# Activation-stationary up projections, two-pass down projections and seven block products for eight in a two-layer fp32 trunk

## The chip, the cores and the metric

The kernel runs on one core of a Trainium2 chip. The metric is the device time of one execution in microseconds (us), as the median of several runs. In the profile PE is TensorE (PEld its weight loads), DVE is VectorE, ACT is ScalarE, POOL is GpSimd and SP is the engine that issues the DMAs. L113 is line 113 of the kernel shown.

## The reference, cut to what matters

Two post-norm layers over 256 positions of 2048 features, all in float32. Layer 0 mixes tokens with a spatial gate (gMLP), layer 1 with latent attention. Each is followed by a gated MLP with a width-3 causal convolution over positions.

```python
def layer_norm(x, g, b):          # over features, in float32
def gmlp_mixer(x, w_in, ln_g, ln_b, w_s, b_s, w_out):
    z = jax.nn.gelu(x @ w_in)                    # 2048 -> 2 * 6144
    u, v = jnp.split(z, 2, axis=-1)
    v = layer_norm(v, ln_g, ln_b)
    ...                                          # s: 128-position windows of v, mixed by masked w_s, plus b_s
    return (u * s.reshape(B, S, GM_HALF)) @ w_out
def conv_ffn(x, w_up, conv_w, conv_b, w_down):
    h = x @ w_up                                 # 2048 -> 2 * 5504
    h = lax.conv_general_dilated(h, ...) + conv_b  # each feature: 3 taps over positions, causal
    a, g = jnp.split(h, 2, axis=-1)
    return (jax.nn.silu(g) * a) @ w_down         # 5504 -> 2048
for i in range(DEPTH):
    m = gmlp_mixer(x, ...) if i % 2 == 0 else mla_mixer(x, ...)
    x = layer_norm(ALPHA * x + m, ...)
    x = layer_norm(ALPHA * x + conv_ffn(x, ...), ...)
```

## The kernel before, in words

Every large product runs as three float32r matmuls. A float32 operand t is split into hi = t rounded to float32r and lo = t - hi; the kernel sums hi·hi, hi·lo and lo·hi. Activations x are split once per layer into four tiles `xhl` ([128 features, 4 blocks, 256 hi + 256 lo positions]). Weights stream from DRAM: class `Feed` holds the list of all weight chunks in their order of use (1 MB each, 128 x 2048). For each, `_load` issues a DMA on SP into a tile `raw`, `_split` makes `wh` with a cast on ScalarE (L75) and `wl` with a subtraction on VectorE (L76), in halves of 1024. `next` is called by the consumer and first brings loads and splits a given number of chunks ahead. All these tiles share one pool `big` of 22 buffers of 8 KB per partition.

The products have two forms. In `prod_b` the activations are the stationary operand and the weights stream, 512 columns at a time; the result is [128 positions, features]. In `prod_a` a 128x128 piece of the weights is stationary and the activations stream: first hi and lo side by side (512 columns) against `wh`, then hi (256 columns) against `wl`; the result is [128 features, positions]. PSUM has eight banks of 128x512, given out in turn.

The stages in order: `v` (six groups of 1024 columns in form b, Gelu, layer norm statistics); `u` (twelve groups of 512 columns in form a, each followed by `gate`, which adds the two halves of a bank, applies Gelu, mixes `v` by a small product `s`, and multiplies); `wo` (`down`: 48 blocks of k, form b, all eight banks as accumulators, both halves of the positions and all 2048 columns); `ffn` of layer 0: `upf` (the first 512 columns, form b, interleaved with the layer norm in `boundary`), then `up` (20 groups of 512 columns in form a, which hold 256 columns of a and the matching 256 of g, and a last half-size group), with `pair` making the convolution, Silu and product for one feature block at a time; `dn` (`down` again, 43 blocks); then the attention; then `ffn` and `dn` of layer 1. The last blocks of k of a `down` are held back (`late`, SKEW) and done bank by bank, so that the layer norm of the first half can run beside them.

Each engine runs its instructions in one written order. A scheduler sets it at build time, engine by engine, from the program and its data dependencies; on the chip it is fixed.

## Time and profile before

| | |
|---|---|
| median of 3 runs | 2559.76 us (2559.61 to 2564.33) |
| the profiled execution | span 2559.8 us |
| PE / DVE / ACT busy | 99% / 61% / 48% |
| granted TensorE clock, mean | 0.998 |
| DMA, mean | 188 GB/s, 52% of the 16 engines' time |
| chain by tile | `up` 36%, `dn` 18%, `u` 10%, `v` 10%, `wo` 10% |

Each row of a group or a timeline names line, engine, operation, output and inputs. The busy time of matmuls is modelled, since they overlap; the distance from one start to the next tells what one costs in a sequence.

### The profile page before, as it was taken

To read this page: it belongs to the slowest core of one execution; us is meant where nothing else is said; L and a number is where in the kernel's file an instruction comes from. 1 tells how busy PE (TensorE), PEld (TensorE's weight loads), DVE (VectorE), ACT (ScalarE), POOL (GpSimd) and SP (SyncE) were. 2 spreads that over 40 slices of the span, in tenths; PEclk is the share of its full clock that TensorE was granted. 3 is DMA by queue.
4 is the path that set the end of the run, shared out by engine and by line. 5 is a ranking of instruction groups with operands and counts; after the bars stand their busy time and mean duration, and the time that the engine had idled before them with its cause. 6 is when DMAs were issued, how large, how long until landed. Compare 5 with 4: busy or idle time off the path is not lost.

```text
span 2559.8 us, 32217 instructions
## 1 busy us (share of the span) xinstructions
PE 2544.2 (99%) x13041; PEld 2152.4 (84%) x13041; DVE 1573.6 (61%) x2284; ACT 1226.4 (48%) x1795; POOL 2.4 (0%) x15
## 2 busy tenths in 40 slices
PE   9999999999999999999999999999999999999998
PEld 7888888888888888888888888877888888888886
DVE  6444675575546766665675547845676576667554
ACT  5434444455443555544554433544365455446441
POOL 0000000000000000000000000000000000000000
PEclk9999999999999999999999999999999999999999
DMA  8545454556563545544565554424555454446552
GB/s 323 194 165 197 165 181 165 181 211 230 200 231 148 214 173 188 182 171 175 198 222 205 205 203 159 165 99 154 191 198 181 163 199 174 184 169 242 206 205 87
DMA packets 68838, 480.18 MB, mean 188 GB/s; under 512 B 7633, under 2 KB 8273, under 8 KB 11729
## 3 DMA queue, kind: packets, MB, share of 16 engines
q1 hardware_dynamic: 68688, 478.13, 52.0%
q8 instruction: 102, 1.67, 0.3%
q14 instruction: 48, 0.39, 0.0%
HBM read 476.00 MB, written 2.10 MB: 187 GB/s over the span
## 4 chain that ended last, share of the span: by engine, by line
PE 99%; DVE 1%; DMA 0%; ACT 0%; issue 0%; SPq 0%; DVEq 0%; ACTq 0%
PE up L113 36%; PE dn L113 18%; PE u L113 10%; PE v L113 10%; PE wo L113 10%; PE mo L113 4%; PE upf L113 2%; PE sc L113 1%; PE mkv L113 1%; PE qn L113 1%; PE kn L113 1%; PE vv L113 1%; PE mq L113 1%; PE s L113 1%; PE qr L113 0%; PE lnt L366 0%
## 5 line engine op out<-in xcount | busy, mean ns | idle before, releaser
L76 DVE TENSOR_TENSOR wl<-raw,wh 128x1024 fp32r<-128x1024 f32 (+2 forms) x886 | 1050.6, 1214 | 473.3 <-ACT wh L75 294.1
L75 ACT CAST wh<-raw 128x1024 fp32r<-128x1024 f32 (+2 forms) x886 | 891.0, 1044 | 523.9 <-DVE wl L76 202.8
L113 PE MATMUL up<-xhl,wh 128*128 128x512 f32 x2624 | 927.5, 399 | 0.0
L113 PE MATMUL up<-xhl,wl 128*128 128x256 f32 x2624 | 737.6, 281 | 0.0
L113 PEld LDWEIGHTS up<-xhl,wh 128*128 128x128 f32 x2624 | 493.5, 188 | 122.6
L113 PEld LDWEIGHTS up<-xhl,wl 128*128 128x128 f32 x2624 | 496.5, 189 | 0.1
L113 PE MATMUL u<-xhl,wh 128*128 128x512 f32 x768 | 268.8, 397 | 0.0
L113 PE MATMUL u<-xhl,wl 128*128 128x256 f32 x768 | 212.2, 279 | 0.0
L113 PE MATMUL v<-wh,xhl 128*128 128x512 f32 x768 | 208.2, 392 | 1.8 <-ACT wh L75 1.8
L113 PE MATMUL wo<-wh,woa 128*128 128x512 f32 x768 | 194.5, 390 | 0.0
L113 PE MATMUL dn<-wh,dn1a 128*128 128x512 f32 x688 | 174.2, 389 | 0.0
L113 PE MATMUL dn<-wh,dn0a 128*128 128x512 f32 x688 | 173.5, 390 | 0.0
L113 PEld LDWEIGHTS v<-wh,xhl 128*128 128x128 f32 x768 | 145.1, 189 | 33.1 <-ACT wh L75 2.3
L113 PEld LDWEIGHTS u<-xhl,wh 128*128 128x128 f32 x768 | 143.5, 188 | 32.8
L113 PEld LDWEIGHTS wo<-wh,woa 128*128 128x128 f32 x768 | 144.1, 188 | 29.8
L113 PEld LDWEIGHTS dn<-wh,dn0a 128*128 128x128 f32 x688 | 129.1, 188 | 26.8
L113 PEld LDWEIGHTS dn<-wh,dn1a 128*128 128x128 f32 x688 | 129.1, 188 | 26.7
L113 PEld LDWEIGHTS u<-xhl,wl 128*128 128x128 f32 x768 | 144.7, 188 | 1.1
L113 PE MATMUL v<-wl,xhl 128*128 128x512 f32 x384 | 119.0, 391 | 0.0
L113 PE MATMUL wo<-wl,woa 128*128 128x512 f32 x384 | 107.0, 390 | 0.0
L113 PE MATMUL dn<-wl,dn1a 128*128 128x512 f32 x344 | 96.0, 389 | 0.0
L113 PE MATMUL dn<-wl,dn0a 128*128 128x512 f32 x344 | 95.2, 390 | 0.0
(204 smaller groups left out, 2113.5 us busy)
## 6 DMA issues: line engine op xcount, KB each, us to landing
raw<-in_ffn_up_dram SPq DMA_DIRECT2D x172, 1024.0 KB, 4.8
raw<-in_gm_in_dram SPq DMA_DIRECT2D x95, 1024.0 KB, 4.7
raw<-in_ffn_dn_dram SPq DMA_DIRECT2D x86, 1024.0 KB, 4.7
raw<-in_gm_wout_dram SPq DMA_DIRECT2D x48, 1024.0 KB, 4.8
raw<-in_ml_out_dram SPq DMA_DIRECT2D x16, 1024.0 KB, 4.8
raw<-in_ml_b_dram SPq DMA_DIRECT2D x14, 1024.0 KB, 4.9
raw<-in_ml_kv_dram SPq DMA_DIRECT2D x5, 864.0 KB, 4.7
lng<-in_ln_rows_dram SPq DMA_DIRECT2D x4, 1024.0 KB, 6.3
```

The lines of the kernel that those rows point to most:

```text
L75: self.nc.scalar.copy(hi[:, c], raw[:, c])
L76: self.nc.vector.tensor_tensor(lo[:, c], raw[:, c], hi[:, c].bitcast(F32), ALU.subtract)
L113: nc.tensor.matmul(o, l, r, start=start, stop=stop, skip_group_check=True)
```

## The change

The weights now come as `Step`s of two blocks of k by 1024 columns, and `square` computes a 1024-column group with activations stationary in four accumulator banks (two halves of the positions by two of the columns). This covers `v`, `u` (six groups instead of twelve) and the 20 groups of `up` (now ten of 1024, hence ten groups per layer numbered 0 to 9). `u` and `up` then have their results in [positions, features], and TensorE transposes them: 16 transposes a group, into banks `uT` or `ht`. The convolution takes two feature blocks of a and two of g at once: 12 scaled copies on ScalarE from PSUM, then two shifted additions of 4 x 255 and 4 x 254 columns on VectorE (`conv3`).

`down` makes two passes over k, one for each half of the columns, the second in reverse order; activations are split again where the second pass needs them. The residual is kept in DRAM meanwhile (`park`, `residual`).

In 115 steps (tables GROUP_V, GROUP_U, GROUP_UP, SEVEN_WO, SEVEN_DN: 15 in `v`, 12 in `u`, 40 in `up`, 16 in `wo`, 32 in both `dn`) the 2x2 by 2x2 block product is done with seven block products by sums of blocks (Winograd's form of Strassen's). Sums of the activations are made once (`sums2`, VectorE, then cast and subtraction); sums of the weights (`wt`) for each step. So such a step has the tiles `wh`, `wl` (1536 columns) and `th`, `tl` (2048). Four more banks `p` gather the products that serve several outputs; `gather` and `out` add them up in a tile `h` or `u`.

```diff
+    def _split(self):
+        ...
+        if s.seven:
+            cols = 1536
+            t = self._tile("wt")
+            last = raw[:, 1536:2048].rearrange("p (n c) -> p n c", n=1).to_broadcast([P, 2, 512])
+            nc.vector.tensor_tensor(t[:, 0:1024]..., raw[:, 512:1536]..., last, ALU.subtract)          # L92
+            t1, b22 = (t[:, 512:1024], raw[:, 512:1024]) if s.by_k else (t[:, 0:512], raw[:, 1024:1536])
+            nc.vector.tensor_tensor(t[:, 1024:1536], b22, t1, ALU.add)                                # L95
+            nc.vector.tensor_tensor(t[:, 1536:2048], raw[:, 0:512], t[:, 1024:1536], ALU.subtract)    # L96
-        step = 512 if i == 0 else 1024 if cols == 2048 else cols // 2
+        step = 512 if self.split == 0 else cols
         for o in range(0, cols, step):
             c = slice(o, o + step)
+            nc.scalar.copy(s.hi[:, c], raw[:, c])                                                     # L100
+            nc.vector.tensor_tensor(s.lo[:, c], raw[:, c], s.hi[:, c].bitcast(F32), ALU.subtract)     # L101
+        if s.seven:
+            s.th, s.tl = self._tile("th", F32R), self._tile("tl", F32R)
+            nc.scalar.copy(s.th, t)                                                                   # L104
+            nc.vector.tensor_tensor(s.tl, t, s.th.bitcast(F32), ALU.subtract)                         # L105
...
+TWO = ((0, False), (1, False), (2, True), (4, False), (3, True), (5, False), (6, False), (7, False))
+THREE = ((0, False), (2, True), (1, False), (3, True), (5, False), (4, True), (6, False), (7, False))
+GROUP_V = [NONE] + [THREE] * 5
+GROUP_U = [TWO] * 6
+GROUP_UP = [TWO] * 10
+SEVEN_WO = tuple(range(8, 40, 4))
+SEVEN_DN = tuple(range(8, 40, 4))
...
+            direct(0, 0, x_parts(xs, k0, 0), w(0, 0))          # Square.step, seven: each line 3 matmuls
+            direct(0, 1, sp(3), w(0, 1))
+            self.mm3(self.p[0], first, x_parts(xs, k1, 0), w(1, 0))
+            self.mm3(self.p[1], first, sp(0), t(o1))
+            self.mm3(self.p[3], first, sp(2), t(o3))
+            self.mm3(self.p[2], first, sp(1), t(1024))
+            direct(1, 0, x_parts(xs, k0, 1), t(1536))
...
+    def conv3(layer, tiles, name):
+        c = [tp.tile([P, 4, S], F32, tag="mid", name=f"c{i}_{name}", bufs=MID) for i in range(3)]
+        for i, (F, src) in enumerate(tiles):
+            nc.scalar.activation(c[0][:, i], src, AF.Identity, bias=..., scale=...)                   # L701
+            nc.scalar.activation(c[1][:, i], src, AF.Copy, scale=...)                                 # L702
+            nc.scalar.activation(c[2][:, i], src, AF.Copy, scale=...)                                 # L703
+        y = c[0][:, 0:n]
+        nc.vector.tensor_tensor(y[:, :, 1:S], y[:, :, 1:S], c[1][:, 0:n, 0 : S - 1], ALU.add)         # L705
+        nc.vector.tensor_tensor(y[:, :, 2:S], y[:, :, 2:S], c[2][:, 0:n, 0 : S - 2], ALU.add)         # L706
...
+        for half in range(2):                                   # down
+            order = back_order(n_k, half)
+            ...
+                feed.room = BIG - 8 - (3 if sevens else 0) - (2 if half else 0) + (i // 4 if half else 0)
```

How the change orders the helpers, at three places. First VectorE around the end of an `up` group in layer 0. Before, the parts for one feature block (`h_`, `c_`, `act`) stand between halves of weight splits (`wl`):

```order
L205 TENSOR_TENSOR h_0a_6850<-up_2_0_6684,lo_0a_6848 128x256
L76 TENSOR_TENSOR wl_7011<-raw_6936,wh_7010 128x1024
L461 SCALAR_TENSOR_TENSOR c_0a_6852<-h_0a_6850,cst,c_0a_6852 128x255
L205 TENSOR_TENSOR h_0g_6858<-up_2_2_6686,lo_0g_6856 128x256
L463 SCALAR_TENSOR_TENSOR c_0a_6852<-h_0a_6850,cst,c_0a_6852 128x254
L76 TENSOR_TENSOR wl_7011<-raw_6936,wh_7010 128x1024
```

After, at the end of group 3 (L405 is the drain of the group's last bank, 14 and 16 are the feature blocks; `wt`, `wl`, `tl` are those of the seven step that comes third in group 4):

```order
L405 TENSOR_TENSOR h_3_7195<-h_3_7195,up_3_1_1_7025 128x512
L705 TENSOR_TENSOR c_0_14_7309<-c_0_14_7309,c_0_14_7310 128x4x255
L706 TENSOR_TENSOR c_0_14_7309<-c_0_14_7309,c_0_14_7311 128x4x254
L718 TENSOR_TENSOR act_1_6681<-s_14_7326,c_0_14_7309 128x512
L705 TENSOR_TENSOR c_0_16_7339<-c_0_16_7339,c_0_16_7340 128x4x255
L706 TENSOR_TENSOR c_0_16_7339<-c_0_16_7339,c_0_16_7341 128x4x254
L718 TENSOR_TENSOR act_2_7356<-s_16_7357,c_0_16_7339 128x512
L92 TENSOR_TENSOR wt_7366<-raw_7237 128x1024
L95 TENSOR_TENSOR wt_7366<-raw_7237,wt_7366 128x512
L101 TENSOR_TENSOR wl_7365<-raw_7237,wh_7364 128x1536
L96 TENSOR_TENSOR wt_7366<-raw_7237,wt_7366 128x512
L105 TENSOR_TENSOR tl_7373<-wt_7366,th_7372 128x2048
```

Both convolutions stand ahead of the weight sums and of the seven step's `wl`. Next ScalarE at the same place. Before, each copy or convolution start alternates with half a weight cast:

```order
L203 COPY lo_0a_6848<-up_2_0_6684 128x256
L75 CAST wh_7010<-raw_6936 128x1024
L460 ACTIVATE c_0a_6852<-h_0a_6850,cst 128x256
L203 COPY lo_0g_6856<-up_2_2_6686 128x256
L75 CAST wh_7010<-raw_6936 128x1024
L460 ACTIVATE c_0g_6860<-h_0g_6858,cst 128x256
```

After, the end of the 24 scaled copies of group 3, then the seven step's casts (`s_16` is the second Silu):

```order
L701 ACTIVATE c_0_16_7339<-ht_3_1_1_7330,cst 128x256
L702 ACTIVATE c_0_16_7340<-ht_3_1_1_7330,cst 128x256
L703 ACTIVATE c_0_16_7341<-ht_3_1_1_7330,cst 128x256
L717 ACTIVATE s_16_7357<-c_0_16_7339 128x512
L100 CAST wh_7364<-raw_7237 128x1536
L104 CAST th_7372<-wt_7366 128x2048
L100 CAST wh_7403<-raw_7268 128x2048
```

The cast `wh_7364` stands behind the second Silu, which needs VectorE's adds. Last, VectorE within `wo`. Before, two weight halves and one activation split (`woa`) for each block of k:

```order
L76 TENSOR_TENSOR wl_5193<-raw_5128,wh_5192 128x1024
L212 TENSOR_TENSOR woa_5154<-pT_2881,woa_5154 128x256
L76 TENSOR_TENSOR wl_5193<-raw_5128,wh_5192 128x1024
L76 TENSOR_TENSOR wl_5228<-raw_5163,wh_5227 128x1024
L212 TENSOR_TENSOR woa_5189<-pT_2881,woa_5189 128x256
```

After, in the second pass, one seven step (five rows of `wt`, `wl`, `tl`) and one plain one, with the split of four blocks of activations:

```order
L92 TENSOR_TENSOR wt_5168<-raw_5057 128x1024
L95 TENSOR_TENSOR wt_5168<-raw_5057,wt_5168 128x512
L101 TENSOR_TENSOR wl_5167<-raw_5057,wh_5166 128x1536
L96 TENSOR_TENSOR wt_5168<-raw_5057,wt_5168 128x512
L105 TENSOR_TENSOR tl_5175<-wt_5168,th_5174 128x2048
L101 TENSOR_TENSOR wl_5179<-raw_5088,wh_5178 128x2048
L92 TENSOR_TENSOR wt_5238<-raw_5139 128x1024
L299 TENSOR_TENSOR woa_5_5233<-v_936,woa_5_5233 128x4x256
```

The `tl` stands directly behind the last row of its `wt`, with ScalarE's cast `th` between them.

## The prediction

> **What bounds the kernel now.** I read the page first, then TensorE's waits, the chain in order of time, the groups by shape, and short stretches of the timelines.

> ```profile
> span 2559.8 us, 32217 instructions
> PE 2544.2 (99%) x13041; PEld 2152.4 (84%) x13041; DVE 1573.6 (61%) x2284; ACT 1226.4 (48%) x1795; POOL 2.4 (0%) x15
> ```

> ```profile
> PE v L113 <- ACT wh L75: 1.8, 1, 1.8
> PE o L113 <- ACT pts L681: 1.5, 1, 1.5
> ```

> TensorE is never late: its longest waits are 1.8 and 1.5 us in the whole span. So time is the sum of its instructions, and VectorE (61%) and ScalarE (48%) only have to be early. The profiled span, 2559.8 us, is within 0.1 us of the median of the runs, 2559.76, so I sum against it.

> The chain gives what each kind of matmul takes when they follow one another (start, length, what):

> ```profile
> 98.70 174.13 PE v L113 x768
> 855.93 457.92 PE up L113 x2592
> 1313.86 231.21 PE dn L113 x1020
> 843.49 0.44 PE lnt L366 x4
> ```

> With activations stationary (`v`, `dn`) one 512-column matmul takes 174.13/768 = 231.21/1020 = 0.2267 us. With weights stationary (`up`) a pair, 512 and 256 columns, takes 457.92/1296 = 0.3533, against 1.5 x 0.2267 = 0.3400 for the same columns in the other form. A 128x128 transpose takes 0.11.

> The helpers' prices are distances from one start to the next, VectorE first, then ScalarE:

> ```profile
> 571.65 0.42 DVE L437 TENSOR_TENSOR pT<-u,sg 128x256 f32<-128x256 f32 x1
> 571.99 1.22 DVE L76 TENSOR_TENSOR wl<-raw,wh 128x1024 fp32r<-128x1024 f32 x1
> 573.12 0.41 DVE L212 TENSOR_TENSOR woa<-pT,woa 128x256 fp32r<-128x256 f32 x1
> ...
> 821.28 0.69 DVE L343 BATCH_NORM_STATS2 lnst<-res 128x6 f32<-128x512 f32 x1
> 821.88 0.73 DVE L355 SCALAR_TENSOR_TENSOR res<-res,lnrs,lnb 128x512 f32<-128x512 f32 x1
> ```

> ```profile
> 855.75 0.56 ACT L460 ACTIVATE c_0a<-uph,cst 128x256 f32<-128x256 f32 x1 [5.28 <-PE uph L490]
> 856.22 0.56 ACT L460 ACTIVATE c_0g<-uph,cst 128x256 f32<-128x256 f32 x1
> ...
> 862.55 0.42 ACT L476 ACTIVATE s<-c_0g 128x256 f32<-128x256 f32 x1
> 862.87 1.99 ACT L75 CAST wh<-raw 128x1024 fp32r<-128x1024 f32 x2
> ...
> 872.14 1.06 ACT L75 CAST wh<-raw 128x1024 fp32r<-128x1024 f32 x1
> 873.09 0.60 ACT L460 ACTIVATE c_0a<-h_0a,cst 128x256 f32<-128x256 f32 x1
> 873.60 0.36 ACT L203 COPY lo_0g<-up 128x256 f32<-128x256 f32 x1
> 873.85 1.06 ACT L75 CAST wh<-raw 128x1024 fp32r<-128x1024 f32 x1
> ```

> VectorE: 0.34 us for 256 columns, 0.60 for 512, 1.13 for 1024, so by the line through them 1.67 for 1536 and 2.2 for 2048. ScalarE: 0.95 for a cast of 1024, so 1.4 and 1.8 for 1536 and 2048; Identity of 256 from PSUM 0.47, a plain copy of 256 0.25, Silu 0.32 (0.54 for 512 by the casts' slope). The new scaled copies of 256 have no row; the plain copy bounds them below, the Identity above. I take 0.33.

> **TensorE's own work.** A seven step takes 7 block products of 3 matmuls where a plain one takes 8: 115 x 3 = 345 fewer, -78.2 us. All of `u` (768 pairs) and 2 x 1280 pairs of `up` change form: 3328 x (0.3533 - 0.3400) = -44.3. Their results are now [positions, features] and have to be turned: 16 transposes in each of 6 `u` and 20 `up` groups, 416 x 0.11 = +45.8. Net -76.7. If nothing waited, 2483.

> **What the helpers must now do.** A plain step (two blocks of k) gives TensorE 24 x 0.2267 = 5.44 us and costs VectorE 2.2. A seven step gives 21 x 0.2267 = 4.76 and costs VectorE, for `wt`, `wl`, `tl`: 1.13 + 0.60 + 0.60 + 1.67 + 2.2 = 6.2, and `tl` must wait until ScalarE has cast the finished `wt` (1.8). On average this fits, but both queues run in their written order, and what counts is who is late at a seven step.

> **Up groups, 10 per layer.** Take the end of group 3 (the order above), t = 0 at its last matmul. VectorE's four drains end at 1.5; the turned banks stand at about 1.7 to 2.3. ScalarE then makes 12 scaled copies for the first two pairs of features (4 x 0.47 + 8 x 0.33 = 4.4): 6.1. VectorE's two shifted adds (1020 columns, 1.13 each): 8.5. Silu, product: 9.8. The last 8 of the next 12 copies had to wait for Silu: 12.2. Adds 14.5, Silu 15.1. Only now comes the cast of the seven step's `wh` (1.4): 16.5, while VectorE ends its product and `wt` at 17.5 and `wl` (1.67) at 19.2. TensorE has done its transposes and the two plain steps, 2.3 + 10.7, at 13.0: it waits about 6 us for `wl`, then about 2 for `th`, the next cast and `tl`. With 0.5 at the drains the group takes 8.6 us more than its work. Groups 5 and 7 stand in the same order; group 1 has a 2.2 us `wl` between its drains too: 10.0. In groups 0 and 2 `wt` comes ahead of the adds and `wl` between the two pairs: 2.3 at the drains and 1.4 at the seven step, 3.7 each. In 4 and 6 `wl` stands ahead of all adds: 1.0 each; group 8: 2.0. The first group waits 2.5 for the same chain on the held-back tiles. After the last, the tail product covers until 13.5, but the down pass's first activations are cast behind that chain, both tail copies and two weight casts, at 21.5: 8.9 with its drains. Sum per layer 35.8 + 7.4 + 2.0 + 2.0 + 2.5 + 8.9 = 58.6; both 117. With the copies at 0.25 and every second-order wait left out it is 76, with 0.47 and one late load per group 135.

> **Down projections.** Six half passes, each with eight seven steps alternating with plain ones: TensorE 10.2 us a pair; VectorE 6.2 + 2.2 + 1.13 (a split of activations each pair) + 1.3 (sums every second) = 10.9, and 1.8 idle for `th` unless other work stands there. The order shows such fillers in about half of the places: 12 a pair. Seven pairs behind the first owe 7 x 1.8 = 13, of which about 8 lie after the last `wl`: 5 a half, 30 together. With every place filled it is 7 x 0.7 less the lead, some 1.5 a half or 9; with none and no overlap of two seven steps 13 or 80. I stay near the low end, since half of the places are seen to be filled.

> **`v`, `u`, start.** `v` needs 37 us of VectorE for 41.5 of TensorE; its room shrinks by a buffer each group and only the last (the seven step's split stands behind the drain) waits, about 4, the rest 1, the start 2: +7 (2 to 15). `u` groups cover their seven steps (TensorE has 5.3 us of transposes and `s` products ahead of two plain steps): 0.5 each. But the first stands behind

> ```profile
> L411 DVE TENSOR_SCALAR v<-v,vmv,vrs 128x1024 f32<-128x1024 f32 x12 | 8.8, 804 | 0.0
> ```

> 12 x 0.73: `wl` at 17.9 where TensorE is ready at 10.9: 7. Together +10 (5 to 15). The boundaries gain a head start by the first pass and lose nothing I can see: 0. Parking the residual in DRAM moves 2 MB a time beside a DMA load of half the span: 0 (to +5).

> **The clock.** TensorE's waits may cost beyond themselves. The stretches (length, busy time of PE, PEld, DVE, ACT, POOL, granted clock, DMA share, GB/s) show it:

> ```profile
> 6.00:9.00 3.00, 1.19 (x5) 0.67 (x4) 0.79 (x2) 1.35 (x3) 0.00 (x0) 1.00 0.85 297
> 9.00:12.00 3.00, 3.00 (x9) 2.35 (x9) 2.24 (x5) 1.43 (x4) 0.00 (x0) 0.58 0.99 404
> 12.00:15.00 3.00, 3.00 (x13) 2.36 (x13) 1.55 (x2) 2.63 (x4) 0.00 (x0) 0.85 1.07 429
> 1690.00:1695.00 5.00, 4.06 (x21) 2.92 (x22) 2.84 (x8) 4.32 (x9) 0.00 (x0) 1.00 0.11 43
> ```

> The 1.8 us wait at the start was followed by clocks of 0.58 and 0.85: 3 x 0.42 + 3 x 0.15 = 1.7 us lost. The 0.9 us idle at 1690 cost none. I count 19 waits above 1.8 us: 0 to 32 us. The start came after a few us of work only, these after ten or more, so I take 6, near the low end.

> [...] This case's start fell after less than 2 us. [...]

> **Sum.** 2559.8 - 76.7 + 117 + 30 + 7 + 10 + 6 = 2653.

> **Rivals.** *The chain is hidden (faster).* One mechanism: the copies, adds and Silus of a group's end are through, and `wl` written, by the time TensorE has done two plain steps. `wl` would have to come at 13.0, not 19.2, in groups 1, 3, 5 and 7. That 2.2 + 2.2 us of adds and 24 copies are real work speaks against it; that VectorE has 36 us of work in a 44 us group speaks for it. Without the 117: 2536. Break-even is where all waits together come to 77, that is 24 instead of 117 here.
> *The halves of the down passes get no lead.* If the buffers let no `wt` start before the last seven step is released, each pair costs 12.8 on VectorE: 8 x 2.6 less 5 = 16 a half, not 5: 2719. For it speaks the room, 8 to 10 buffers, where a seven step holds 4, a plain one 2 and the next needs 3 beside its raw; against it that VectorE, once late, finds the buffers free.
> *The clock falls at every long wait:* 32 instead of 6: 2679.

> **How the numbers follow.** No change is within 0.2% here, 5 us, about what runs of this kernel can tell. My forecast (waits of 100 to 220 us) 0.55, no lead 0.15, clock 0.10: all slower, 0.80. Hidden chain 0.17, whole range below 2555. The same 0.03: the gain and waits would have to match by chance. Low sums take 76 + 9 + 2 + 5 of waits: 2575; high ones 135 + 80 + 15 + 15 + 32: 2760. The range 2580 to 2725 takes in the rival without lead and leaves out the hidden chain and the last of the high side, about 2 in 10.

> **What would show it.** TensorE busy some 2480 us with idle time of 130 us or more; waits of `up` for `wl` (L101) and `wh` (L100) of 5 us and more, four times a layer, and under 1 us in groups 4 and 6; one wait of 8 us at each `dn`'s start and one of 7 in `u`'s first group; matmuls of 0.227 in `up`. I'm wrong if `up`'s groups last 44 us each, if PE stays at 99%, or if the waits are on DMA (raw), which I priced at nothing.

## The result, and the profile after

The changed kernel takes 2725.28 us (median, 2724.64 to 2729.11), before 2559.69: ratio 1.0644, 95% interval 1.0629 to 1.0659. It is slower, as forecast, but by 166 us, not 93: the value lies at the very upper end of the range (2580 to 2725), 0.3 us past it. The profiled execution has a span of 2723.1 us.

The page of after, first lines:

```profile
span 2723.1 us, 29502 instructions
PE 2559.9 (94%) x11448; PEld 2051.3 (75%) x11448; DVE 2123.5 (78%) x2028; ACT 1443.9 (53%) x1573; POOL 2.4 (0%) x15
```

TensorE went from 99% to 94%, and VectorE from 1574 to 2124 us. TensorE's waits (us in total, times, longest):

```profile
PE up L167 <- ACT wh L100: 34.8, 25, 3.5
PE up L167 <- DVE wl L101: 14.3, 12, 1.9
PE dn L167 <- ACT wh L100: 12.7, 23, 0.6
PE ht L756 <- DVE h L405: 11.3, 8, 1.8
PE dn_p L167 <- ACT th L104: 10.1, 18, 0.9
PE lnt L612 <- DVE res L601: 9.6, 4, 4.6
PE dn L167 <- ACT dn1a L298: 8.7, 1, 8.7
PE dn L167 <- ACT dn0a L298: 8.3, 1, 8.3
PE u L167 <- DVE wl L101: 5.6, 1, 5.6
```

TensorE waits on no DMA: the late ones are the weight helpers (`wh`, `wl`, `th`), the drains of `up` (`h`), the first activations of `dn`, and the layer norm (`lnt`), which the prediction didn't name. Short waits are undercounted in such rows: a matmul is drawn 0.39 us long where one starts every 0.2267, so the first 0.16 us of each is hidden. So I compare stages by starts, from the first matmul of one to the first of the next (us):

| stage | before | forecast | after |
|---|---|---|---|
| `v` | 267.0 | 263.8 | 262.1 |
| `u` | 289.6 | 291.8 | 295.5 |
| `wo` | 262.9 | 262.0 | 275.2 |
| boundary (`upf`) | 24.6 | 24.6 | 30.1 |
| `up` with the entry into `dn`, layer 0 / 1 | 464.0 / 464.0 | 509.5 | 513.1 / 515.1 |
| `dn`, layer 0 / 1 (to the end) | 235.5 / 244.5 | 234.6 / 243.6 | 253.6 / 263.7 |
| attention, with `mq` | 276.8 | 276.8 | 281.8 |
| second `upf` | 25.2 | 25.2 | 27.3 |

The forecast column is the prediction's sum laid on the stages (for `up` 464.0 - 17.1 - 13.6 + 17.6 + 58.6), without the 6 for the clock; it sums to 2647 with the 5.6 before the first matmul. Of the 76 us between it and the span, 52 are in the three down projections and 13 at the boundaries (the one ahead of the attention lies within its row); `v`, `u` and each `up` came within 6.

**The down passes.** VectorE in the second pass of `dn`, layer 0 (start, length, what, idle time before):

```profile
1542.33 2.29 DVE L105 TENSOR_TENSOR tl<-wt,th 128x2048 fp32r<-128x2048 f32 x1 [2.05 <-ACT th L104]
1544.54 2.28 DVE L101 TENSOR_TENSOR wl<-raw,wh 128x2048 fp32r<-128x2048 f32 x1
1546.75 1.22 DVE L299 TENSOR_TENSOR dn0a<-act,dn0a 128x1024 fp32r<-128x1024 f32 x1
1547.88 1.21 DVE L92 TENSOR_TENSOR wt<-raw 128x1024 f32<-128x1024 f32 x1
1549.13 0.69 DVE L95 TENSOR_TENSOR wt<-raw,wt 128x512 f32<-128x512 f32 x1
1549.74 1.75 DVE L101 TENSOR_TENSOR wl<-raw,wh 128x1536 fp32r<-128x1536 f32 x1
1551.41 0.68 DVE L96 TENSOR_TENSOR wt<-raw,wt 128x512 f32<-128x512 f32 x1
1554.12 2.29 DVE L105 TENSOR_TENSOR tl<-wt,th 128x2048 fp32r<-128x2048 f32 x1 [2.03 <-ACT th L104]
```

A pair of steps takes 1554.12 - 1542.33 = 11.8 us where TensorE has 10.2 of work, and 2.03 of it VectorE stands idle: the last row of `wt` (L96) comes behind `wl`, ScalarE can cast `th` only then, and `tl` is next in VectorE's queue.

**The groups of `up`.** The chain of the prediction's walk, at the end of group 3, whose last matmul starts at 1065.0; all engines:

```profile
1079.60 0.63 ACT L717 ACTIVATE s<-c 128x512 f32<-128x512 f32 x1 [2.25 <-DVE c L706]
1080.13 1.46 ACT L100 CAST wh<-raw 128x1536 fp32r<-128x1536 f32 x1
1081.64 0.50 PE L167 MATMUL up<-wh,xhl 128*128 128x512 f32 x1 [3.49 <-ACT wh L100]
1082.73 1.75 DVE L101 TENSOR_TENSOR wl<-raw,wh 128x1536 fp32r<-128x1536 f32 x1
1084.53 0.79 PE L167 MATMUL up<-wl,xhl 128*128 128x512 f32 x1 [1.91 <-DVE wl L101]
```

With t = 0 there `wh` comes at 16.6 and `wl` at 19.5 (16.5 and 19.2 in the walk). The granted clock in two stretches there, and over the groups 3 and 4 together (columns as in the prediction):

```profile
1079.00:1082.40 3.40, 0.76 (x3) 0.48 (x3) 2.67 (x4) 1.99 (x2) 0.00 (x0) 1.00 0.85 288
1082.40:1089.20 6.80, 4.89 (x12) 3.34 (x12) 4.83 (x4) 4.09 (x3) 0.00 (x0) 0.50 0.01 4
1017.30:1117.90 100.60, 92.57 (x406) 73.75 (x405) 77.14 (x63) 58.93 (x75) 0.00 (x0) 0.97 0.48 167
```

Behind the wait the clock is 0.50 for 6.8 us. The trace has 15 stretches at half speed, not counting the one at the very end, 106 us in all; they hold 53 us less of work than at full speed. The prediction gave the clock 6 us.

**The boundaries.** VectorE at the end of `wo`, within the layer norm that TensorE's transposes `lnt` wait for:

```profile
829.33 2.27 DVE L101 TENSOR_TENSOR wl<-raw,wh 128x2048 fp32r<-128x2048 f32 x1
...
832.24 0.74 DVE L600 SCALAR_TENSOR_TENSOR res<-res,lnmv,lng 128x512 f32<-128x512 f32 x1
832.90 2.28 DVE L101 TENSOR_TENSOR wl<-raw,wh 128x2048 fp32r<-128x2048 f32 x1
835.10 0.15 DVE L268 RECIPROCAL lnrs<-lnrs_0q 128x1 f32<-128x1 f32 x1
```

Two weight splits of 2.3 us stand inside the norm's chain. Counted from the start of the kernel (each step makes one `wl`, the first one four), they belong to the first chunks of the next stage, `upf`.

### The profile page after: what moved, and what is told of

It reads as the page before. It is cut to its first block, busy times and chain, and to the rows that moved or that the text cites. A ratio compares the mean times of both kernels' runs of the same rounds, so it can differ in the third digit from the quotient of the medians.

```text
span 2723.1 us, 29502 instructions
## 1 busy us (share of the span) xinstructions
PE 2559.9 (94%) x11448; PEld 2051.3 (75%) x11448; DVE 2123.5 (78%) x2028; ACT 1443.9 (53%) x1573; POOL 2.4 (0%) x15
## 4 chain that ended last, share of the span: by engine, by line
PE 54%; DVE 15%; ACT 10%; issue 8%; DMA 1%; DVEq 0%; ACTq 0%; SPq 0%
PE up L167 18%; PE u L167 8%; PE dn L167 6%; DVE wl L101 5%; PE wo L167 4%; PE mo L167 3%; PE up_p L167 3%; ACT wh L100 2%; DVE wt L92 2%; ACT th L104 2%; ACT c L701 2%; PE upf L167 2%; ACT c L702 1%; ACT c L703 1%; PE sc L167 1%
## 5 line engine op out<-in xcount | busy, mean ns | idle before, releaser
L101 DVE TENSOR_TENSOR wl<-raw,wh 128x2048 fp32r<-128x2048 f32 (+2 forms) x447 | 939.3, 2116 | 59.9 <-ACT wh L100 51.1
L100 ACT CAST wh<-raw 128x2048 fp32r<-128x2048 f32 (+2 forms) x447 | 786.2, 1777 | 228.6 <-DVE wl L101 62.5
L167 PE MATMUL up<-wh,xhl 128*128 128x512 f32 x2000 | 568.3, 395 | 35.1 <-ACT wh L100 34.8
L104 ACT CAST th<-wt 128x2048 fp32r<-128x2048 f32 x115 | 220.2, 1915 | 496.6 <-DVE wt L96 467.3
L167 PEld LDWEIGHTS up<-wh,xhl 128*128 128x128 f32 x2000 | 374.7, 189 | 125.9 <-ACT wh L100 50.9
L105 DVE TENSOR_TENSOR tl<-wt,th 128x2048 fp32r<-128x2048 f32 x115 | 263.5, 2291 | 183.6 <-ACT th L104 183.6
L167 PE MATMUL up<-wl,xhl 128*128 128x512 f32 x1000 | 316.2, 394 | 14.3 <-DVE wl L101 14.3
L167 PEld LDWEIGHTS up<-wl,xhl 128*128 128x128 f32 x1000 | 187.7, 189 | 59.4 <-DVE wl L101 21.3
L167 PE MATMUL u<-wh,xhl 128*128 128x512 f32 x600 | 165.0, 390 | 0.0
L92 DVE TENSOR_TENSOR wt<-raw 128x1024 f32<-128x1024 f32 x115 | 139.9, 1217 | 0.6 <-PE wo L167 0.6
L167 PEld LDWEIGHTS wo<-wh,woa 128*128 128x128 f32 x544 | 101.3, 188 | 30.1 <-ACT wh L100 9.7
L167 PEld LDWEIGHTS dn<-wh,dn1a 128*128 128x128 f32 x464 | 87.1, 190 | 38.6 <-ACT wh L100 11.9
L167 PEld LDWEIGHTS dn<-wh,dn0a 128*128 128x128 f32 x464 | 86.9, 190 | 38.5 <-ACT wh L100 12.2
L405 DVE TENSOR_TENSOR h<-h,up 128x512 f32<-128x512 f32 x80 | 51.3, 683 | 73.3 <-PE up L167 72.5
```

What stands on the lines that cost most here:

```text
L92: nc.vector.tensor_tensor(t[:, 0:1024].rearrange("p (n c) -> p n c", n=2), raw[:, 512:1536].rearrange("p (n c) -> p n c", n=2), last, ALU. ...
L100: nc.scalar.copy(s.hi[:, c], raw[:, c])
L101: nc.vector.tensor_tensor(s.lo[:, c], raw[:, c], s.hi[:, c].bitcast(F32), ALU.subtract)
L104: nc.scalar.copy(s.th, t)
L105: nc.vector.tensor_tensor(s.tl, t, s.th.bitcast(F32), ALU.subtract)
L167: nc.tensor.matmul(o, l, r, start=start, stop=stop, skip_group_check=True)
```

## The experiments

Theories: the waits come from the order in which VectorE and ScalarE do the helpers (mine); from VectorE's amount of work; from buffers or loads; or from the slow clock behind each wait. Where a ratio is given it is to before on the same chip.

**The seven steps of `up` later.**

```diff
-GROUP_UP = [TWO] * 10
+GROUP_UP = [((0, False), (1, False), (4, False), (5, False), (2, True), (6, False), (3, True), (7, False))] * 10
```

> Same work; in each group of `up` the two seven steps stand fifth and seventh instead of third and fifth. Theory A (the chain at a group's end, 24 scaled copies, adds, Silus, then `wl`, is longer than two plain steps): with four plain steps (21.8 us) ahead of it the chain is covered, the long groups (52.7 us in layer 0: the 2nd, 4th, 6th and 8th after the first) fall to about 45, the half-speed stretches inside `up` go, and the time falls by 50 to 70 us, to 2655 to 2675. Theory B (VectorE with its waits for `th` is full in `up`, 42 of 44 us a group, so lateness only moves to a later step): groups still average 49 us, the time stays at 2715 to 2735.

2689.29 us, 1.0494 (1.0478 to 1.0511): 36 less, neither theory's number. ScalarE at the same place, and TensorE's wait:

```profile
1070.13 0.63 ACT L718 ACTIVATE s<-c 128x512 f32<-128x512 f32 x1 [2.25 <-DVE c L707]
1070.67 5.06 ACT L100 CAST wh<-raw 128x2048 fp32r<-128x2048 f32 x3
PE up L168 <- ACT wh L100: 33.2, 8, 4.2
```

The chain is as long as it was; now the `wh` of the third, plain step stands behind it, since splits run only two steps ahead.

**Down projections without seven steps** (`SEVEN_WO = SEVEN_DN = ()`).

> No seven steps in the three down projections: 48 x 3 matmuls more, +33 us of TensorE work. Theory A (VectorE, 9.7 us of work and 2.05 us of waiting for `th` a pair of steps, is what TensorE waits for there): VectorE needs under 7 us for two plain steps of 10.9, the waits inside the passes (some 55 us in the three stages) go, those at the end of each second pass (5 us each) stay, some 5 us of half-speed clock go: 2690 to 2705. Theory B (the buffers and the late weight loads hold the down passes): the waits stay and the work is added: 2745 to 2760.

2669.38 us, 1.0417 (1.0399 to 1.0434), less than theory A's range. With 33 us more work it is 56 us faster, so the seven steps there cost about 89 us of waits. `wo` takes what it took before with as many matmuls (262.1 us, before 262.9), and the wait at the boundary behind it, which I had expected to stay, is gone too (25.1): all four splits of `upf` now stand ahead of the norm's rows. The bytes loaded are the same, but the passes also have 3 buffers more of room, so this run alone doesn't rule out the buffers; the next one does for the passes.

**Sums ahead of `wl`.**

```diff
-            nc.vector.tensor_tensor(t[:, 1536:2048], raw[:, 0:512], t[:, 1024:1536], ALU.subtract)
+            ready = nc.vector.tensor_tensor(t[:, 1536:2048], raw[:, 0:512], t[:, 1024:1536], ALU.subtract)
...
+            with self.tc.issue_after(ready.ins):      # VectorE: wl behind the last row of wt
+                nc.vector.tensor_tensor(s.lo[:, 0:cols], raw[:, 0:cols], s.hi[:, 0:cols].bitcast(F32), ALU.subtract)
```

> Same work; in every seven step VectorE now does all three sums of weights (`wt`) first and `wl` behind them, so that ScalarE casts `th` while VectorE does `wl`, and `tl` finds it ready. Theory A (the 2 us that VectorE stands idle for `th` in each of 99 seven steps is what makes it late in the down passes): VectorE's waits for `th` fall from 184 us to under 60, a pair of steps in a down pass takes 10.3 to 10.8 us instead of 11.8 to 12.35, and the time falls by 30 to 55 us: 2670 to 2695; nearly nothing of it in `up`, where the chain ahead of `wl` is the same. Theory B (VectorE's work itself, or the buffers, hold the passes): idle time moves to other places, the time stays within 10 us of 2725.

2640.02 us, 1.0303 (1.0284 to 1.0323): 85 less, more than theory A's range. VectorE's waits for `th`, after and here:

```profile
DVE tl L105 <- ACT th L104: 183.6, 99, 3.5
```

```profile
DVE tl L102 <- ACT th L101: 36.9, 90, 4.1
```

VectorE in a down pass here:

```profile
1516.79 2.29 DVE L102 TENSOR_TENSOR tl<-wt,th 128x2048 fp32r<-128x2048 f32 x1 [0.37 <-ACT th L101]
...
1524.80 1.75 DVE L100 TENSOR_TENSOR wl<-raw,wh 128x1536 fp32r<-128x1536 f32 x1
1526.92 2.29 DVE L102 TENSOR_TENSOR tl<-wt,th 128x2048 fp32r<-128x2048 f32 x1 [0.37 <-ACT th L101]
```

The same instructions, with the same buffers, take 10.1 us a pair. `wo` falls from 275.2 to 257.3, `dn` from 253.6 and 263.7 to 232.4 and 241.8: 61 of the 85 us. `up` gains 10 and 9. The boundary behind `wo` stays at 30.0 us although `wo` is 18 us shorter, and the two splits still stand in the norm's chain:

```profile
806.10 2.27 DVE L109 TENSOR_TENSOR wl<-raw,wh 128x2048 fp32r<-128x2048 f32 x1
...
809.67 2.28 DVE L109 TENSOR_TENSOR wl<-raw,wh 128x2048 fp32r<-128x2048 f32 x1
```

So that wait goes with the place of these splits in the queue, and not with a late pass.

**The clock by itself.** A kernel that leaves the computation out: streams of 512-column matmuls with waits between them; one run.

> Leaves the whole computation out: streams of 66 to 121 matmuls of 512 columns, and between them waits for a chain on VectorE that grows from about 1.2 to 6 us in steps of 0.35, eight of each. Theory A (the trace of the changed kernel: in a fixed grid of 3.41 us stretches, one with more than about 2.1 us of idle TensorE is followed by half speed): no fall after waits under 2.1 us; after waits of 2.2 to 2.6 in about 4 or 5 of 10, of 3.0 to 3.4 in about 7 of 10, after all above 4.2. Theory B (only a wholly idle stretch of 3.4 us halves the clock): none under 3.4 us, 2 in 10 at 4.1, 7 in 10 at 5.8. Theory C (any wait above 1.8 us does): all from 1.9 us on.

Falls to half speed, eight waits of each length (us):

| wait | 1.5 | 2.0 | 2.5 | 2.9 | 3.4 | 3.9 and more |
|---|---|---|---|---|---|---|
| followed by half speed | 0 | 3 | 0 | 2 | 6 | all |

The 2.0 includes one of 1.9. A wait of 2.02 from 434.59 on, and one of 2.94 from 487.80 on, in stretches of 3.413 us, each with what follows (all changes of the granted clock in this trace lie whole multiples of 3.413 us apart, as do the 31 in the trace of the changed kernel):

```profile
434.64:438.05 3.41, 1.55 (x7) 1.23 (x7) 1.61 (x4) 0.00 (x0) 0.00 (x0) 1.00 0.02 5
438.05:441.46 3.41, 3.41 (x9) 2.64 (x8) 0.00 (x0) 0.00 (x0) 0.00 (x0) 0.50 0.00 0
...
485.84:489.25 3.41, 2.12 (x10) 1.43 (x8) 1.18 (x3) 0.00 (x0) 0.00 (x0) 1.00 0.00 0
489.25:492.66 3.41, 1.92 (x9) 1.63 (x10) 1.28 (x4) 0.00 (x0) 0.00 (x0) 1.00 0.00 0
492.66:496.07 3.41, 3.41 (x17) 2.83 (x16) 0.00 (x0) 0.00 (x0) 0.00 (x0) 1.00 0.00 0
```

The first lies in one stretch, and the next has a clock of 0.50; the longer one is shared by two, and the clock stays at 1.00. Counted from matmul to matmul, stretches at full clock with up to 1.86 us of idle time never led to a fall, those with 2.43 and more always did; in between (1.95 to 2.12) four of eleven did. That is theory A with the limit near 2.0 in this run, where the idle time of a stretch alone doesn't settle it. Its shares by length were not met (none at 2.5): the grid cut these eight waits so that none had more than 2.07 us in one stretch. At 2.0 theory B has no fall and theory C eight; three were measured.

**TensorE kept busy in the waits of `up`.**

```diff
+                for _ in range(15):                    # ahead of the first seven step, groups 2, 4, 6, 8
+                    mm(o, idle[:, 0:P], idle, False, False)
+                mm(o, a[0], b[0], False, False)
+                for _ in range(6):
+                    mm(o, idle[:, 0:P], idle, False, False)
```

> The changed kernel itself, with TensorE kept busy in the eight long waits of `up`: 15 bf16 matmuls that add zero ahead of the first seven step of groups 2, 4, 6 and 8, and 6 behind its first matmul (0.21 us each, 3.2 and 1.3 us, within the waits of 3.0 to 3.5 and 1.25 to 1.9). No helper is touched. Theory A (the half-speed stretches behind these waits cost their full loss, 3.4 us each and 30 in all): 2692 to 2700. Theory A' (some of the loss lies where TensorE would wait for `th` and `tl` anyway, about 1.2 us of each 3.4): 2704 to 2712. Theory B (VectorE sets the pace there, the slow clock costs nothing): 2718 to 2728. In A and A' the half speed inside these groups is gone; if it is still there, the fall doesn't come from the wait.

2726.80 us, 1.0643 (1.0622 to 1.0664): no change. The groups 3 and 4 here, from the same transposes to the same transposes as the stretch of 100.60 us above:

```profile
1021.60:1122.20 100.60, 95.54 (x426) 74.21 (x426) 77.15 (x63) 58.89 (x75) 0.00 (x0) 1.00 0.48 167
```

At full clock the two groups take the same 100.60 us. The time that TensorE gains it spends in short waits for helpers (its waits for `th` in `up` rise from 1.8 to 8.8 us): VectorE and ScalarE set the period, and the slow clock lay in it.

**The other long waits filled** (25 such matmuls in the first `u` group, 38 at each `dn` entry, 20 at two boundaries).

> The changed kernel itself, with TensorE kept busy by bf16 matmuls whose results aren't used or add zero (0.21 us each), in its other long waits: 25 in the first `u` group (wait 5.6 us), 38 at each `dn` entry (8.3 and 8.7), 20 ahead of the layer norm's transposes at the boundaries behind `wo` and the first `dn` (4.6). No helper is touched. The half-speed time behind these waits is 6.8, 10.2 and 10.2, and 3.4 to 10.2 us long. Theory A (a slow clock costs its full loss here, since TensorE has four plain steps ahead of it that nobody holds up): 3.4 + 2 x 5 + 5, some 18 us less, 2705 to 2711. Theory A' (real where TensorE is the bound behind the wait, in `u` and at the boundaries; in the down passes VectorE's pace takes it back): 2713 to 2719. Theory B (nothing, as in the groups of `up`): 2722 to 2728.

2723.01 us, 1.0616 (1.0600 to 1.0632), after 1.0644 (1.0629 to 1.0659). Half speed is gone from `u` and both entries and shorter at the boundaries. `u` gains 2.6 us (295.5 to 292.9), the last `dn` with its `up` 1.9; the first `dn` with its `up` loses 1.7, and no other stage moves by more than 1. That is theory B's range. The times differ by 2.3 us, the ratios by 0.28%, 7 us, with intervals that meet: going by the medians of the two runs with filled waits, the clock itself cost some 7 us of the 53 at most.

**Three steps of lead in `up`**, on top of the two edits (sums first, seven steps later): `feed.next(splits=3)`.

> The order of sums of the run with `wl` behind `wt` (2640), the seven steps of `up` fifth and seventh, and `up` now lets the splits run three steps ahead instead of two (same work). Theory A (what is left in `up` is one chain per group, 24 copies, adds, Silus, then the next cast `wh` or `wl`; with three plain steps split before it TensorE has 18.4 us of cover, and the chain ends 17 to 18 us after the group): the waits of 2 to 4 us in the groups go and with them the half-speed stretches there; each `up` stage falls from 503 to 506 us to 465 to 470, the time to 2560 to 2585. Theory B (a helper is late somewhere in each group whatever the order, as when the seven steps alone were moved and a plain step's `wh` came 4.2 us late instead): one wait of 2 to 4 us per second group stays, 2595 to 2615.

2627.37 us, 1.0255 (1.0232 to 1.0278): a miss, above even theory B's range. The waits for `wh` and `wl` in `up` are nearly gone, but the one for the drains, 11.3 us in the changed kernel, is now TensorE's longest in total:

```profile
PE ht L761 <- DVE h L410: 40.8, 22, 4.3
```

**Three more places mended:** first `u` group late, `dn`'s first activations split ahead of the tail, the norm's first rows ahead of splits in halves.

```diff
+GROUP_U = [LATE2] + [TWO] * 5                      # LATE2: the later order above
+        hl = {0: split4(act[0], 0, 4, f"dn{layer}a0_0")}        # ahead of the tail of up
+        with tc.high_priority(offset=500):                      # start and scale of the first norm rows
+        step = 512 if self.split == 0 else 1024 if s.ks is None and cols == 2048 else cols
```

> As the kernel of this batch with three steps of lead, and three more places mended, same work: the first `u` group has its seven steps fifth and seventh; the first activations of each `dn` are split before the tail of `up`; at the stage boundaries the layer norm's first rows go ahead of weight splits, which come in halves of 1024. If each wait is a cost of its own place (theory A): -9 in `u` (5.6 of wait, 3.4 of clock), -8 to -11 at each `dn` entry, -4 to -7 at two boundaries: 33 to 45 us below the kernel with three steps of lead alone, about 2520 to 2545 and so faster than before. Theory B (the helpers have no slack there either, the buffers taken early stop weight loads in the tail): under 20 us.

2617.35 us, 1.0217 (1.0200 to 1.0233): 10 less, as in theory B. `u` gained 4.9, the entries' waits fell from 7.8 to 4.5 each, the boundary stayed at 29.3. The drains still wait; VectorE at the end of a group:

```profile
1208.22 4.49 DVE L109 TENSOR_TENSOR wl<-raw,wh 128x2048 fp32r<-128x2048 f32 x2
1212.62 2.48 DVE L410 TENSOR_TENSOR h<-h,up 128x512 f32<-128x512 f32 x4
```

The lead that was to help has put two splits ahead of the drains.

**The third split behind the drains.**

```diff
+            z = square(..., 2).out(f"h{layer}_{g}")
+            if g < 9:
+                feed.ahead(feed.used + 3, feed.used + 3)
```

> As the kernel with all places mended, but in `up` the third step of the next group is split behind the group's drains instead of ahead of them: VectorE's `wl` then stands between the drains and the convolution's adds, where VectorE waits for the scaled copies. Theory A (the 40 us of waits for the drains `h`, 2 to 4.3 us a group, came from two `wl` of 2.2 us standing ahead of them): these waits go, groups take 44.5 to 46 us instead of 47 to 51, 2565 to 2590. Theory B (the group period is set by VectorE's and ScalarE's own chain, as with the filled waits, where nothing was gained): the wait moves once more, 2600 to 2620.

2563.24 us, 1.0003 (0.9994 to 1.0012): 54 less, beyond theory A's range.

```profile
1151.65 2.47 DVE L410 TENSOR_TENSOR h<-h,up 128x512 f32<-128x512 f32 x4
1154.04 2.28 DVE L109 TENSOR_TENSOR wl<-raw,wh 128x2048 fp32r<-128x2048 f32 x1
1158.09 1.22 DVE L711 TENSOR_TENSOR c<-c,c 128x1020 f32<-128x1020 f32 x1 [1.77 <-ACT c L708]
```

The `wl` now fills a wait that was there anyway, and TensorE's wait for the drains falls from 40.5 us in 20 waits to 8.6 in 16. Groups of layer 0 take 44.3 to 45.7 us (45 to 51 before this edit), `up` 466.6 and 466.3. The matmuls are those of the changed kernel, and so are the helpers but for 46 weight splits that are done in halves. The ratio went from 1.0644 to 1.0003, so nearly all of the changed kernel's loss was the order and the time of its helpers.

**No seven steps at all,** in the mended kernel before this last edit.

> The kernel with all places mended, without any seven step: activations stationary, transposes, two passes. 345 matmuls more, +78 us of TensorE work; VectorE has 4.2 us less to do per replaced step. Theory A (once nothing waits for it, a seven step is worth its 0.68 us): 55 to 78 us above the mended kernel with seven steps, less what waits that one still has; about 2560 to 2600, that is near before (2560), since the new form and the transposes cancel (-44 and +46). Theory B (seven steps cost in waits what they save, in any order): within 15 us of the mended kernel.

2584.53 us, 1.0090 (1.0070 to 1.0110): 33 below its own kernel, against theory A; it misses in the other direction from theory B too, since there the seven steps of `up` still cost more than they saved. Against the kernel with the split behind the drains, 1.0003, the seven steps are worth 0.9% or some 22 us, of 78 in matmuls.

**The mix:** `up` as before, the rest mended, with seven steps in `v`, `u`, `wo`, `dn`.

> A mix: `up` in the form of before (weights stationary, pairs of features, no seven steps, no transposes; 464 us a stage before), everything else as in the kernel with all places mended (seven steps in `v`, `u`, `wo` and `dn`, sums ahead of `wl`). If the stages are worth what each had in its own run (theory A: v 258, u 290, wo 257, `up` 464 twice, dn 226 to 232 and 236, boundaries and attention as mended), the sum is 2535 to 2555, below before (2560). Theory B (the buffers that the down passes and their seven steps need, or a convolution with fewer small buffers, make `up` or the entries late): 2560 to 2585.

2546.18 us, 0.9939 (0.9925 to 0.9952), within theory A's range: this form beats both kernels, the one before by 0.6%, as the stages foretold (`v` 258.0, `u` 289.5, `wo` 256.8, `up` 464.0 twice, `dn` 229.5 and 239.3). Its page:

```profile
span 2544.4 us, 31767 instructions
PE 2507.2 (99%) x12528; PEld 2104.9 (83%) x12528; DVE 1980.9 (78%) x2360; ACT 1341.8 (53%) x1575; POOL 2.4 (0%) x15
```

**The mix with four steps held back** (`LATE = 4`).

> The mix (2546), with four steps held back at the end of each `down` and of the attention's output instead of three: TensorE then has 10.9 instead of 8.2 us of matmuls beside the layer norm of the first half of the positions. Theory A (the 4.1 us wait for its rows at two boundaries is a matter of cover): 2 x 2.7 us and some half speed less, 2537 to 2543. Theory B (the fourth step holds two more buffers, weight splits for the next stage come later): 2545 to 2552.

2553.92 us, 0.9959 (0.9945 to 0.9973): no gain, and just above theory B's range; the intervals overlap, so a loss isn't shown either.

## Why the prediction was right in direction and 72 us short

**TensorE's own work, -76.7: right.** The two traces differ by just the sum's matmuls and transposes: 345 products fewer, 3328 pairs in the other form, 416 transposes more. The busy time that the prediction named as a sign, 2480, read 2559.9, mostly since half-speed matmuls count as busy (53 us); the idle time, 163 us, was as named (130 or more).

**Up groups, 117: nearly right, 126.** The walk held to 0.3 us, and the group behind it took 52.7 us for 186 x 0.2267 + 16 x 0.11 = 43.9 of work, 8.8 lost (forecast 8.6). From transposes to transposes, the losses behind the groups 0 to 8 of layer 0 were 4.0, 10.2, 4.0, 8.8, 0.9, 8.8, 1.7, 8.8 and 2.5 us; the forecast was 3.7, 10.0, 3.7, 8.6, 1.0, 8.6, 1.0, 8.6 and 2.0. For a long group the prediction saw a wait of 6 us and 2 of small ones; measured were 5.4 of wait and 3.4 of half speed in place of the small ones. That sum is no accident: the fill shows that the helpers' chain fixes the period. Copies took 0.36 us (0.33 assumed). The entries (8.3 and 8.7, forecast 8.9 with drains) and the first `u` group (5.6, forecast 7) were where it put them; `v` and `u` together came to 19, forecast 17.

**Down projections, 30: the step that failed, 82.** The three stages took 50 us longer than before, with 33 us less of matmuls. The rate was right, 12 us a pair against 11.9 to 12.5 on average in the six passes, though partly by luck: VectorE stood idle for `th`, 2.0 us, in all pairs of the second passes and most of the first, not in half. Wrong was "of which about 8 lie after the last `wl`: 5 a half": seven pairs at 12.2 instead of 10.2 come to 14 us, and 13.7 a half were paid, so nothing was given back. The rival without lead had nearly the size (16 a half), but its reason, the buffers, was wrong: with the same buffers the other order of sums took away 61 us. The row that showed the fault, `tl` directly behind the last row of `wt`, had been read; it was priced as a wait that fillers cover, and not as one that a swap of two rows would remove.

**Boundaries, 0: 13.** "The boundaries gain a head start and lose nothing I can see" took for granted that VectorE is free at a pass's end. At the first one the norm's rows stand behind splits for the next stage: where these came ahead of the norm the boundary took 25.1 us, and where they stayed in its chain 30.0, though the pass had become 18 us shorter.

**The clock, 6: near by luck, wrong in the reason.** Half speed came behind nearly all the long waits, as in the rival (32 us), and took 53 us of TensorE's pace, but in the two runs with filled waits nearly all of it cost nothing (some 7 us at most). In the run on the clock about 2.0 us of idle time within one stretch of 3.413 us was enough for half speed in the next. The fall at the start of the kernel before fits that too: the wait there, 1.8 us in its row, is 2.2 us long when counted from matmul to matmul, and lies in one stretch.

Open: why the splits for the next stage stand in the norm's chain when the passes have seven steps; in the mended kernel, in halves, some still do, and the boundary takes 29 to 30 us (24.6 before). Of the 56 us that the seven steps lose even in the best order, the stages of the two runs tell the place but not the cause: `v` keeps 9.9 of its 10.2 us, `u` and `wo` about half, each `up` some 5 of 13.6, the two `dn` nothing, and the boundary and the attention lose 4.5 and 6.8.

## What to carry to other kernels

When one engine is to be relieved at the cost of helpers, walk the helpers' written queues around each place where the bound engine turns to their product, and look for an instruction that stands directly behind its own round trip over another engine: swapping it with an independent neighbour gave 85 us here, and putting a split between drains and adds another 54, in a later version. More lead isn't the same as better order: running splits further ahead put them in front of the drains. Before pricing a slow clock, ask whether the engine behind it is the one that sets the period.
